# Sixteen-head sparse attention: the even heads' probabilities transposed in squares and by DMA, their product with the values one pair later

## The chip, the cores and the metric

One core of a Trainium2 chip runs the whole program. The metric is device time in microseconds (us) of one execution, the median of three runs. TensorE (PE) does the matrix products, with its weight load shown apart (PEld); VectorE (DVE) and ScalarE (ACT) do everything else that touches elements; GpSimd (POOL) and SyncE (SP) here only start transfers.

## The reference

Two layers and a last norm over x (512 tokens by 2048). Layer 0 is a causal convolution beside a block attention of 8 heads (MoBA). Layer 1 is the sparse attention (DSA) that the change is in:

```python
    q = (cq @ w_qb).reshape(b, t, DSA_HEADS, DSA_HEAD_DIM)
    q_lat = jnp.einsum('bthd,hdc->bthc', q, w_uk)
...
        score = jnp.where(kpos[None, :] <= qpos[:, None], score, -jnp.inf)
        sel = lax.top_k(score, k_top)[1]
...
        p = jax.nn.softmax(s.astype(jnp.float32), axis=-1).astype(kv.dtype)
        return jnp.einsum('bqhk,bqkc->bqhc', p, kv)
...
    o = jnp.einsum('bthc,hcd->bthd', o_lat, w_uv).reshape(b, t, DSA_WIDTH)
    return (o * jax.nn.silu(gate)) @ w_out
```

There are 16 heads of 128, 512 tokens, 128 selected keys for each query. All is in float32.

## The kernel before

Every float32 product is three products of rounded halves (`mm3`, lines 87 to 89): high by low, low by high, high by high. Each operand of one is split by `split` (lines 96 and 97): ACT rounds it to the high part, DVE subtracts for the low part. Weights are loaded by SP in 256 KB pieces and split the same way.

The order of instructions on each engine is fixed at build time. The code gives each piece a due time with `at(t)`, and a planner takes, at each moment of its own simulated clock, the ready instruction with the earliest due time; on the chip each engine then goes through its queue in that order, so an instruction that waits holds up all behind it. Tiles come from pools of a few buffers by tag (`BUFS`): `C` has 8, three of them held by the selection masks, `u` 4, `pt` 7, `A1`, `A2` and `Y` 16 each. The PSUM tags have 2 (`g`), 2 (`s`), 3 (`x`) and 1 (`o`) banks.

The DSA stage goes through 8 pairs of heads, 2 D = 19.8 us of due time each (lines 722 to 769). A pair projects the values v for both heads (24 products 256 wide, two tiles split into four `A2` tiles), then for each head k (6 products 512 wide) and q (12), and calls `attention` (line 223): in four chunks c of 128 queries, scores against 128 (c + 1) keys, the mask and row minimum on DVE (line 238), the exponential with its sum on ACT (line 240), a reciprocal and the normalising multiply on DVE (lines 241, 242), and 10 transposes of 128 by 128 on PE into PSUM (line 249). Three PSUM banks are split into `pt` tiles, and `mm3` takes their product with v (`pso`). The result is multiplied by the head's gate (line 765) and split into `Y` and `A1` tiles, which the last matrix (`w_out2`) reads.

The MoBA stage already has a second way for 7 of its 8 heads, `turned` and `turned_values` (lines 267 to 312): DVE transposes each chunk in 32 by 32 squares into the tile `turn0` (line 286), 16 DMAs of 64 KB started from POOL move the squares to their places in `turn1` (line 290), and one head later `turned_values` splits `turn1` on ACT and DVE and multiplies by v. There is one `turn0` and one `turn1`. The first ACT instruction of that split is made to wait for a named matmul (`behind`).

Of the kernel before, what the change touches and what calls it, by code (L numbers as in the profile page):

```python
# [7 lines left out]
F32R = mybir.dt.float32r  # L8
I32 = mybir.dt.int32
AF = mybir.ActivationFunctionType  # L10
OP = mybir.AluOpType
# [3 lines left out]
P = 128  # L15
# [8 lines left out]
HO = 16  # L24
# [15 lines left out]
def f32(ap):  # L40
    return ap.bitcast(F32)


class Builder:
# [219 lines left out]
            self.mm3(po[:, j * P:], vh, vl, parts[b][0][:, o:o + n], parts[b][1][:, o:o + n], j == 0, j == NT - 1)  # L264
        return po

    def turned(self, q, k, bias, ts):


        nc = self.nc  # L270
        z, y = self.turn
        for c in range(NT):
            w = P * (c + 1)
            self.at(ts(c))
            ps = self.psum("s")
            cs = slice(c * P, (c + 1) * P)
            self.mm3(ps[:, :w], q[0][:, cs], q[1][:, cs], k[0][:, :w], k[1][:, :w], True, True)
            p = self.s("u")
            mn, sm = self.s("col", (P, 1)), self.s("col", (P, 1))
            nc.vector.tensor_tensor_reduce(out=p[:, :w], in0=ps[:, :w], in1=bias(c), scale=1.0, scalar=-OUT,  # L280
                                           op0=OP.add, op1=OP.min, accum_out=mn)
            nc.scalar.activation(p[:, :w], p[:, :w], AF.Exp, bias=mn, scale=-1.0, accum_out=sm)
            nc.vector.reciprocal(sm, sm)
            nc.vector.tensor_scalar(p[:, :w], p[:, :w], sm, None, op0=OP.mult)

            nc.vector.transpose(z[:, :, c, :c + 1, :], p[:, :w].rearrange("p (j b x) -> p b j x", b=4, x=32))  # L286

        for a in range(4):
            for b in range(4):
                nc.gpsimd.dma_start(y[32 * b:32 * (b + 1), a], z[32 * a:32 * (a + 1), b])  # L290
# [171 lines left out]
    def values(self, g, tags=("gg", "xx")):  # L462

        out = []
        for b in range(2):
            t0 = self.t
            ps = [self.psum(tag) for tag in tags[b]]
            for k in range(KC):
                wh, wl = self.weights(self.d["w_v"][g, k], t0 + 1.3 * k)
                self.at(t0 + 1.3 * k)  # L470
                xh, xl = self.xs[k]
                for i in range(2):
                    cs = slice((2 * b + i) * P, (2 * b + i + 1) * P)
                    self.mm3(ps[i], xh[:, cs], xl[:, cs], wh, wl, k == 0, k == KC - 1)
            self.t = t0 + 1.3 * KC
            self.at(self.t)
            for i in range(2):
                j = 2 * b + i
                vh, vl = self.s("G", dt=F32R), self.s("G", dt=F32R)
                self.split(ps[i], vh, vl, self.rcol[:, j:j + 1])  # L480
                out.append((vh, vl))
        return out
# [135 lines left out]
    def odd(self):  # L618
        nc, d = self.nc, self.d
# [4 lines left out]
        ps = self.gemm(d["w_ikw"], self.xs, m=m)  # L624
# [4 lines left out]
        for c in range(NT):  # L629
# [10 lines left out]
                                       op0=OP.mult, op1=OP.mult)  # L640
# [4 lines left out]
        ilh, ihl = self.s("T", dt=F32R), self.s("T", dt=F32R)  # L645
# [4 lines left out]
        h0, zh = self.s("T", dt=F32R), self.s("T", dt=F32R)  # L650
# [5 lines left out]
        gates = []  # L656
# [12 lines left out]
        for i in range(HI // 2):  # L669

            ps = self.gemm(d["w_iq"][i], [(a[:, KTOP:], b[:, KTOP:]) for a, b in cq], n=T - KTOP)
            for e in range(2):
                h = 2 * i + e
# [6 lines left out]
                for c in range(1, NT):  # L680
                    w = P * (c + 1)
# [9 lines left out]
                    else:  # L691
                        nc.vector.scalar_tensor_tensor(sc[c][:, :w], rl[:, :w], iw[:, c, h:h + 1], sc[c][:, :w],
                                                       op0=OP.mult, op1=OP.add)
# [23 lines left out]
        def bias(c):  # L717
            return self.cmask[:, T - P:] if c == 0 else sc[c][:, :P * (c + 1)]

        self.ys = []  # L720
        D = 9.9
        for pair in range(HO // 2):
            t0 = self.t
            wv, wk, wq0, wq1 = [self.weights(d["w_qk"][pair, :, 512 * i:512 * (i + 1)], t0 + (0, 2.6, 3.9, 12.5)[i])
                                for i in range(4)]
            self.at(t0)
            v = []
            for b in range(2):
                ps = self.psum("g")
                for a in range(2):  # L730
                    c = 2 * b + a
                    for k in range(2):
                        cs = slice(c * P, (c + 1) * P)
                        ws = slice(256 * k, 256 * (k + 1))
                        self.mm3(ps[:, 256 * a:256 * (a + 1)], ckv[k][0][:, cs], ckv[k][1][:, cs],
                                 wv[0][:, ws], wv[1][:, ws], k == 0, k == 1)
                vh, vl = self.s("A2", dt=F32R), self.s("A2", dt=F32R)
                self.split(ps, vh, vl)
                v.append((vh, vl))
            for e in range(2):  # L740
                h = 2 * pair + e
                th = t0 + D * e + (0 if e else 2.6)
                parts = []
                for i, (w, xs, o) in enumerate(((wk, ckv, 256 * e), ((wq0, wq1)[e], cq, 0))):
                    self.at(th + 1.3 * i)
                    ps = self.psum("g")
                    for k in range(len(xs)):
                        ws = slice(o + P * k, o + P * (k + 1))
                        self.mm3(ps, w[0][:, ws], w[1][:, ws], xs[k][0], xs[k][1], k == 0, k == len(xs) - 1)
                    zh, zl = self.s("A2", dt=F32R), self.s("A2", dt=F32R)  # L750
                    if i:
                        nc.scalar.activation(zh, ps, AF.Copy, scale=-SCALE)
                        nc.vector.scalar_tensor_tensor(zl, ps, -SCALE, f32(zh), op0=OP.mult, op1=OP.subtract)
                    else:
                        self.split(ps, zh, zl)
                    parts.append((zh, zl))
                k, q = parts

                def vj(j):
                    o = 256 * (j % 2) + P * e  # L760
                    return v[j // 2][0][:, o:o + P], v[j // 2][1][:, o:o + P]

                po = self.attention(q, k, vj, bias, lambda c: th + 6.5 + 1.2 * c, lambda c: th + 12 + 1.2 * c, th + 19, "C")
                y = self.s("tmp")
                nc.vector.tensor_tensor(y, po, gates[h], op=OP.mult)
                yh, yl = self.s("Y", dt=F32R), self.s("A1", dt=F32R)
                self.split(y, yh, yl)
                self.ys.append((yh, yl))
            self.t = t0 + 2 * D

    def final(self):
# [145 lines left out]
```

## Time and profile before

| | us |
|---|---|
| median of three runs | 1522.16 |
| lowest and highest | 1520.82, 1522.37 |
| profiled execution, its own time | 1521.33 |
| its span, first to last instruction | 1519.5 |
| start of the first and of the last gate multiply of the DSA pairs (line 765) | 1186.9, 1344.6 |

The 1.83 us between the span and the profiled time lie outside the instructions. The pairs run from about 1160 us to 1345 us of the span; before them the selection masks are made, and after them comes the product with `w_out2`.

### The profile page before, as it was taken

Reading aid. Unit: us, or ns where it says so; the run is one execution under the profiler, and the core shown is the slowest. Engines: PE = TensorE matmul, PEld = TensorE weight load, DVE = VectorE, ACT = ScalarE, POOL = GpSimd, SP = SyncE. Lnnn points to the kernel's source line nnn. Section 1 sums busy time; section 2 is a strip of 40 time slices with the busy share of each in tenths; the row PEclk is TensorE's granted clock in tenths of the full one; section 3 lists DMA queues with packets and bytes.
Section 4 is the critical chain, followed back from the end, with each engine's and each line's share of the span. In section 5 each row is a group of like instructions: output and inputs, shape, how many; then the busy total and the mean of one; then the engine's idle time right before and its main releaser. Section 6 shows DMA issues by size and latency. Waiting matters only on the chain.

```text
span 1519.5 us, 20122 instructions
## 1 busy us (share of the span) xinstructions
PE 1504.2 (99%) x7137; PEld 1261.3 (83%) x7137; DVE 1018.8 (67%) x1980; ACT 677.5 (45%) x1219; POOL 55.5 (4%) x117
## 2 busy tenths in 40 slices
PE   9999999999999999999999999999999999999996
PEld 7888888888888888888888887788888889888886
DVE  7799999976576645664444445557995898843344
ACT  7533333345374534543333333545324666633341
POOL 0000000002022202220000000000000000000000
PEclk9999999999999999999999999999999999999998
DMA  7233333356234733364444332222232111133333
GB/s 234 89 105 114 102 106 102 104 146 173 93 108 132 204 104 115 113 173 138 146 145 145 125 98 85 95 91 78 90 98 91 55 51 49 56 125 118 126 125 112
DMA packets 97397, 173.22 MB, mean 114 GB/s; under 512 B 12112, under 2 KB 18000, under 8 KB 97296
## 3 DMA queue, kind: packets, MB, share of 16 engines
q1 hardware_dynamic: 93280, 164.45, 34.5%
q0 software_dynamic: 3584, 7.35, 1.7%
q8 instruction: 56, 0.92, 0.2%
q14 instruction: 45, 0.37, 0.1%
q10 hardware_dynamic: 432, 0.14, 0.0%
HBM read 153.93 MB, written 10.49 MB: 108 GB/s over the span
## 4 chain that ended last, share of the span: by engine, by line
PE 97%; DMA 1%; DVE 1%; ACT 0%; issue 0%; SPq 0%; DVEq 0%; ACTq 0%
PE psg L87 28%; PE psg L89 28%; PE psg L88 28%; PE psx L87 1%; PE psx L88 1%; PE psx L89 1%; PE psx L249 1%; PE pss L88 1%; PE pss L89 1%; PE pss L87 1%; PE pso L88 1%; PE pso L89 1%; PE pso L87 1%; DMA wr<-in_w_v 1%; DMA C<-in_w_in 0%; PE psx L686 0%
## 5 line engine op out<-in xcount | busy, mean ns | idle before, releaser
L96 ACT ACTIVATE wh<-wr 128x512 fp32r<-128x512 f32 x508 | 319.4, 629 | 652.2 <-PE psg L89 542.1
L97 DVE TENSOR_TENSOR wl<-wr,wh 128x512 fp32r<-128x512 f32 x508 | 348.5, 687 | 296.3 <-ACT wh L96 295.4
L87 PE MATMUL psg<-A,wh 128*128 128x512 f32 (+1 forms) x1328 | 517.0, 390 | 0.2 <-DVE tmp L782 0.2
L88 PE MATMUL psg<-A,wl 128*128 128x512 f32 x1120 | 436.5, 390 | 0.0
L89 PE MATMUL psg<-A,wh 128*128 128x512 f32 x1120 | 436.4, 390 | 0.0
L87 PEld LDWEIGHTS psg<-A,wh 128*128 128x128 f32 (+1 forms) x1328 | 248.7, 187 | 52.8 <-ACT wh L96 0.6
L88 PEld LDWEIGHTS psg<-A,wl 128*128 128x128 f32 x1120 | 209.6, 187 | 44.8 <-issue 0.4
L89 PEld LDWEIGHTS psg<-A,wh 128*128 128x128 f32 x1120 | 209.6, 187 | 44.4 <-issue 0.4
L415 DVE SCALAR_TENSOR_TENSOR C<-u,cst,C 128x512 f32<-128x512 f32 x240 | 170.0, 745 | 0.2
L89 PE MATMUL psg<-Y,wh 128*128 128x512 f32 x336 | 130.9, 390 | 0.0
L88 PE MATMUL psg<-Y,wl 128*128 128x512 f32 x336 | 130.9, 390 | 0.0
L290 POOL DMA_DIRECT2D turn<-turn x112 | 55.0, 499 | 609.0 <-DVE turn L286 459.4
L88 PEld LDWEIGHTS psg<-Y,wl 128*128 128x128 f32 x336 | 63.0, 188 | 13.0
L89 PEld LDWEIGHTS psg<-Y,wh 128*128 128x128 f32 x336 | 63.1, 188 | 12.8
L87 PE MATMUL psg<-T,wh 128*128 128x512 f32 x160 | 62.6, 391 | 0.0
L88 PE MATMUL psg<-G,wl 128*128 128x512 f32 (+1 forms) x160 | 60.7, 379 | 0.0
L89 PE MATMUL psg<-G,wh 128*128 128x512 f32 (+1 forms) x160 | 60.6, 379 | 0.0
L87 PE MATMUL psg<-Y,wh 128*128 128x512 f32 x128 | 49.8, 389 | 0.0
L240 ACT ACTIVATE C<-C,col 128x128 f32<-128x128 f32 (+1 forms) x64 | 35.8, 560 | 15.6 <-DVE col L238 15.2
L87 PE MATMUL psg<-G,wh 128*128 128x512 f32 (+1 forms) x96 | 36.2, 377 | 0.0
L87 PEld LDWEIGHTS psg<-T,wh 128*128 128x128 f32 x160 | 30.0, 188 | 6.1 <-DVE A L97 0.2
L89 PEld LDWEIGHTS psg<-G,wh 128*128 128x128 f32 x160 | 30.1, 188 | 5.1
(316 smaller groups left out, 2137.0 us busy)
## 6 DMA issues: line engine op xcount, KB each, us to landing
wr<-in_w_in SPq DMA_DIRECT2D x268, 256.0 KB, 3.0
wr<-in_w_out SPq DMA_DIRECT2D x128, 256.0 KB, 2.9
wr<-in_w_v SPq DMA_DIRECT2D x64, 256.0 KB, 2.9
wr<-in_w_qk SPq DMA_DIRECT2D x32, 256.0 KB, 2.4
turn<-turn POOLq DMA_DIRECT2D x112, 64.0 KB, 3.9
Y<-in_xT SPq DMA_DIRECT2D x16, 256.0 KB, 5.1
wr<-in_w_pw SPq DMA_DIRECT2D x16, 256.0 KB, 2.9
tmp<-in_xT SPq DMA_DIRECT2D x16, 256.0 KB, 3.0
```

The source lines that it names most:

```text
L87: i = mm(ps, lh, rl, start=start, stop=False)
L88: mm(ps, ll, rh, start=False, stop=False)
L89: mm(ps, lh, rh, start=False, stop=stop)
L96: i = nc.scalar.activation(th, src, AF.Copy)
L97: nc.vector.tensor_tensor(tl, src, f32(th), op=OP.subtract)
L240: nc.scalar.activation(p[:, :w], p[:, :w], AF.Exp, bias=mn, scale=-1.0, accum_out=sm)
L249: nc.tensor.transpose(px[b][:, o:o + P], p[:, j * P:(j + 1) * P], self.ident)
L290: nc.gpsimd.dma_start(y[32 * b:32 * (b + 1), a], z[32 * a:32 * (a + 1), b])
L415: nc.vector.scalar_tensor_tensor(y, u[:, i:i + T], self.c("w_dw", n * TAPS + i), y, op0=OP.mult, op1=OP.add)
```

## The change

In pairs 0 to 6 the first head of the pair (heads 0, 2, ... 12) takes the `turned` way. Its normalising multiply is done by ACT in place of DVE, then DVE transposes squares into `turn0` and 16 DMAs from POOL move them to `turn1`. Its product with v, the gate and the split of the result come in the next pair, due at t0 + 15 (the split at t0 + 13), behind the k projection of that pair's second head. Pair 7 keeps `attention` for both heads, and also takes the product of head 12.

Since v of a pair is now read in the next pair, v goes in turn to four tiles of tag `T` left from the indexer and to four `u` tiles. The results of the first eight finished heads go to `A1`, of the others to `Y`. The second head's projections now stand ahead of the first head's attention in the program text; the due times of both are as they were.

```diff
-    def turned(self, q, k, bias, ts):
+    def turned(self, q, k, bias, ts, ptag="u", scalar=False):
...
-            nc.vector.tensor_scalar(p[:, :w], p[:, :w], sm, None, op0=OP.mult)
+            if scalar:
+                nc.scalar.activation(p[:, :w], p[:, :w], AF.Copy, scale=sm)
+            else:
+                nc.vector.tensor_scalar(p[:, :w], p[:, :w], sm, None, op0=OP.mult)
...
+        places = [[ilh, ihl, h0, zh], [self.s("u", dt=F32R) for _ in range(4)]]
+        self.ys = [None] * HO
+        left = 2 * HO
...
+            yh, yl = [self.s("A1" if left > HO else "Y", dt=F32R) for _ in range(2)]
...
-                vh, vl = self.s("A2", dt=F32R), self.s("A2", dt=F32R)
+                vh, vl = places[pair % 2][2 * b:2 * b + 2]
...
+                    if not i:
+                        self.mid = ins.ins.name
...
+            values = lambda v, e: lambda j: [x[:, 256 * (j % 2) + P * e:][:, :P] for x in v[j // 2]]
+            if late:
+                po = self.turned_values(values(late, 0), t0 + 15, self.mid)
+                finish(2 * pair - 2, po)
+            late = v if pair < HO // 2 - 1 else None
+            for e in range(2):
+                h = 2 * pair + e
+                th = t0 + D * e + (0 if e else 2.6)
+                k, q = qk[e]
+                if late and e == 0:
+                    self.turned(q, k, bias, lambda c: th + 6.5 + 1.2 * c, "C", True)
+                    continue
+                po = self.attention(q, k, values(v, e), bias, lambda c: th + 6.5 + 1.2 * c,
+                                    lambda c: th + 12 + 1.2 * c, th + 19, "C")
+                finish(h, po)
```

## Rows read from the trace of the kernel before

**Rows 1.** The page: busy time by engine, and the chain that ended last.

```profile
PE 1504.2 (99%) x7137; PEld 1261.3 (83%) x7137; DVE 1018.8 (67%) x1980; ACT 677.5 (45%) x1219; POOL 55.5 (4%) x117
...
PE 97%; DMA 1%; DVE 1%; ACT 0%; issue 0%; SPq 0%; DVEq 0%; ACTq 0%
```

**Rows 2.** Stretch, us, busy of PE, PEld, DVE, ACT, POOL; clock, DMA, GB/s.

```profile
1181.00:1301.00 120.00, 120.00 (x738) 107.62 (x737) 107.04 (x296) 79.15 (x193) 0.00 (x0) 1.00 0.16 52
1281.00:1301.00 20.00, 20.00 (x123) 17.74 (x122) 18.63 (x51) 13.55 (x34) 0.00 (x0) 1.00 0.17 54
```

**Rows 3.** Waits from 1161 to 1345 us: total, times, longest; DVE's eight, and PEld's.

```profile
DVE tmp L765 <- PE pso L89: 10.6, 8, 2.7
...
DVE pt L97 <- ACT pt L96: 0.4, 2, 0.2
...
PEld psg L87 <- DVE A L97: 0.4, 2, 0.2
```

**Rows 4.** PE's timeline (start, us, name, count) around transposes, and without them.

```profile
1249.12 0.95 PE L249 MATMUL psx<-ident,C 128*128 128x128 f32 x7
1249.82 0.31 PE L87 MATMUL pss<-A,A 128*128 128x128 f32 x1
1249.96 0.28 PE L88 MATMUL pss<-A,A 128*128 128x128 f32 x1
...
1269.92 0.22 PE L87 MATMUL pso<-pt,A 128*128 128x128 f32 x1
1269.98 0.27 PE L88 MATMUL pso<-pt,A 128*128 128x128 f32 x1
```

**Rows 5.** PE's timeline: the first k product of pair 1 and of pair 6.

```profile
1177.72 0.39 PE L87 MATMUL psg<-T,wh 128*128 128x512 f32 x1
...
1280.86 0.39 PE L87 MATMUL psg<-T,wh 128*128 128x512 f32 x1
1281.09 0.39 PE L88 MATMUL psg<-T,wl 128*128 128x512 f32 x1
```

**Rows 6.** Groups by line, 1161 to 1345 us: busy us, mean ns, idle before.

```profile
L97 DVE TENSOR_TENSOR pt<-psx,pt 128x512 fp32r<-128x512 f32 (+1 forms) x48 | 27.9, 594 | 0.4 <-ACT pt L96 0.4
...
L242 DVE TENSOR_SCALAR C<-C,col 128x128 f32<-128x128 f32 (+1 forms) x64 | 23.8, 381 | 0.8
L96 ACT ACTIVATE pt<-psx 128x512 fp32r<-128x512 f32 (+1 forms) x48 | 23.6, 523 | 6.1 <-PE psx L249 6.0
```

**Rows 7.** Groups by line in the MoBA stage, 340 to 690 us.

```profile
L286 DVE STREAM_TRANSPOSE turn<-u 128x128 f32<-128x128 f32 (+3 forms) x28 | 14.2, 507 | 0.3
...
L97 DVE TENSOR_TENSOR pt<-turn,pt 128x512 fp32r<-128x512 f32 (+3 forms) x28 | 12.7, 484 | 0.6 <-ACT pt L96 0.5
L96 ACT ACTIVATE pt<-turn 128x512 fp32r<-128x512 f32 (+3 forms) x28 | 11.9, 458 | 3.4 <-PE psg L87 3.4
```

**Rows 8.** POOL's timeline: two batches of 16 moves; then their row of DMA issues.

```profile
469.81 1.47 POOL L290 DMA_DIRECT2D turn<-turn  x3 [28.35 <-DVE turn L286]
471.55 6.36 POOL L290 DMA_DIRECT2D turn<-turn  x13 [0.27 <-issue]
...
621.53 3.92 POOL L290 DMA_DIRECT2D turn<-turn  x8 [26.43 <-issue]
...
628.97 2.45 POOL L290 DMA_DIRECT2D turn<-turn  x5 [0.37 <-issue]
...
turn<-turn POOLq DMA_DIRECT2D x112, 64.0 KB, 3.9
```

**Rows 9.** Timelines of pairs 4 and 5: normalising multiplies, second head's last k group.

```profile
1253.21 0.54 DVE L242 TENSOR_SCALAR C<-C,col 128x128 f32<-128x128 f32 x2
...
1258.39 0.48 DVE L242 TENSOR_SCALAR C<-C,col 128x512 f32<-128x512 f32 x1
...
1268.09 0.48 PE L87 MATMUL psg<-T,wh 128*128 128x512 f32 x1
...
1275.65 0.28 DVE L242 TENSOR_SCALAR C<-C,col 128x128 f32<-128x128 f32 x1
```

More of the change, by code (lines that the diff above doesn't have):

```diff
@@ L277, in turned @@
             self.mm3(ps[:, :w], q[0][:, cs], q[1][:, cs], k[0][:, :w], k[1][:, :w], True, True)
-            p = self.s("u")
+            p = self.s(ptag)
             mn, sm = self.s("col", (P, 1)), self.s("col", (P, 1))
@@ L718, in bias, with finish @@
             return self.cmask[:, T - P:] if c == 0 else sc[c][:, :P * (c + 1)]
-        self.ys = []
+        places = [[ilh, ihl, h0, zh], [self.s("u", dt=F32R) for _ in range(4)]]
+        self.ys = [None] * HO
+        left = 2 * HO
+        def finish(h, po):
+            nonlocal left
+            y = self.s("tmp")
+            nc.vector.tensor_tensor(y, po, gates[h], op=OP.mult)
+            yh, yl = [self.s("A1" if left > HO else "Y", dt=F32R) for _ in range(2)]
+            left -= 2
+            self.split(y, yh, yl)
+            self.ys[h] = (yh, yl)
+        late = None
         D = 9.9
@@ L736, in odd @@
                                  wv[0][:, ws], wv[1][:, ws], k == 0, k == 1)
-                vh, vl = self.s("A2", dt=F32R), self.s("A2", dt=F32R)
+                vh, vl = places[pair % 2][2 * b:2 * b + 2]
                 self.split(ps, vh, vl)
                 v.append((vh, vl))
+            qk = []
             for e in range(2):
@@ L748, in odd @@
                         ws = slice(o + P * k, o + P * (k + 1))
-                        self.mm3(ps, w[0][:, ws], w[1][:, ws], xs[k][0], xs[k][1], k == 0, k == len(xs) - 1)
+                        ins = self.mm3(ps, w[0][:, ws], w[1][:, ws], xs[k][0], xs[k][1], k == 0, k == len(xs) - 1)
+                    if not i:
+                        self.mid = ins.ins.name
                     zh, zl = self.s("A2", dt=F32R), self.s("A2", dt=F32R)
@@ L756, in odd @@
                     parts.append((zh, zl))
[L757 to L768, printed above, removed]
+                qk.append(parts)
+            values = lambda v, e: lambda j: [x[:, 256 * (j % 2) + P * e:][:, :P] for x in v[j // 2]]
[13 more added lines that the diff above has]
+                finish(h, po)
             self.t = t0 + 2 * D
```

## The prediction

> **What bounds the kernel now.** I read the page first: which engine is busy, and who owns the chain that ended last. PE is busy 99% of the span and owns 97% of that chain [rows 1]. An average says nothing of one stage, so next come the stretches of the DSA pairs: from 1181 to 1301 us PE is busy 120.00 of 120.00 us at full granted clock [rows 2]. The waits of the stage say the same from the other side: PE's weight load waited 0.4 us for DVE in 184 us, and everything else in the list is an engine that waits for PE or for its own inputs [rows 3]. So PE's queue sets the time here, and a product taken out of it moves the end by its pitch, as long as nothing else becomes late. The engine to watch is DVE: busy 107.04 of 120 us, 89%, and 93% in the densest 20 us, there too without a PE stall [rows 2]. ACT has 66%, POOL nothing.
>
> A pair takes (1280.86 - 1177.72) / 5 = 20.63 us [rows 5].
>
> **What is removed from PE.** Seven heads lose 10 transposes each. A record's length (0.27 us) overlaps its neighbours, so I take start to start: seven transposes move the next product by 1249.82 - 1249.12 = 0.70 us, and the narrow product behind them keeps the one after it waiting 0.14 us where it takes 0.06 us without transposes ahead [rows 4]. That is 0.78 us for seven, 0.11 us each, 1.1 us a head and **7.7 us** for seven heads. The products with v and the scores keep their shapes, they only change places: head 0's values leave pair 0, head 12's enter pair 7. Nothing is added to PE.
>
> **What is added to DVE and ACT**, for each turned head. Out of DVE go four normalising multiplies, 4 x 0.381 = 1.52 us, and three splits from PSUM, 3 x 0.594 = 1.78 us [rows 6]. Into it come four square transposes, 4 x 0.507 = 2.03 us, and four splits of the moved squares, 4 x 0.484 = 1.94 us [rows 7], priced on the same shapes in the MoBA stage. Net +0.67 us. A pair has 0.892 x 20.63 = 18.4 us of DVE now, 19.1 us after, in 20.63 - 1.1 = 19.5 us: 98%. These busy times count the tail of each instruction, which the next one overlaps, so the true fill is lower; still it is the least cover in this change. ACT loses 3 x 0.523 = 1.57 us [rows 6] and gains four splits, 4 x 0.458 = 1.83 us [rows 7], and four multiplies that the trace doesn't show; bounded by 0 and by the 0.523 us of a PSUM split, I take 0.458 us, the nearest in shape, 1.83 us. Net +2.1 us a pair on 0.66 x 20.63 = 13.6 us: 80% full, not a bound by itself.
>
> **The moves.** One head's 16 moves are issued in 477.91 - 469.81 = 8.1 us at best and 631.42 - 621.53 = 9.9 us at worst of these two batches, and the last lands a median 3.9 us later [rows 8]: 12 to 14 us. Nothing else is in POOL's queue in the pairs [rows 2], so no issue is moved past another there; SP's queue keeps its weight loads. The added traffic is 1 MB a pair beside 52 GB/s [rows 2], another 1 MB / 19.5 us = 54 GB/s; I cost it at nothing, since loads are due 8 us ahead. If that cover were gone, a weight split would be late, and PE with it.
>
> What waits on the moves is the tight place. In pair 4 the first head's last normalising multiply ends at 1258.87 us [rows 9]. After the change an ACT multiply and a transpose stand there, about 1.3 us more, so POOL starts near 1260.7 and the squares are landed at 1273 to 1275. Two instructions of pair 5 need that. The split on ACT may start once the k group at 1268.09 us has run [rows 9], 1.1 us earlier with the shorter pair, so 1267: the guard by itself lets it go 6 to 8 us too soon. Only the planner's own idea of a landing, and the due time t0 + 13 behind more urgent work, keep it back. And the first transpose of pair 5 overwrites the tile that the moves read; its place is that of the multiply at 1275.65 us [rows 9], about 1274.8 after: just as the moves end, with -0.2 to 1.8 us to spare. Behind a DVE instruction that waits there stand the weight splits that PE needs next.
>
> The buffers: v now lives in tiles that no one else uses in the pairs, and `Y` slots come free with the gates, two for each head finished. I cost these at nothing; the work that would be late if I am wrong is the split of v, which PE needs last in the pair.
>
> **The sum.** PE -7.7 us. For new stalls I take 0 to 0.2 us for each of six pairs as the likeliest, +0.7 us: the densest stretch ran at 93% of DVE without one [rows 2]. The profiled 1521.33 us (its span 1519.5 us and 1.83 us around it) becomes 1514.3 us, and the median, 0.83 us above it, 1515.1 us. This case's own range: 1514.0 (no stall, and transposes in small groups cost a little more than 0.11 us) to 1518.
>
> **Rival 1: DVE becomes the bound.** DVE now waits 28.9 us in 184 us (eight rows [rows 3], the greatest 10.6 us for the product with v), 3.2 us in each pair. With 19.1 us of work in 19.5 us these waits must almost vanish. Most do by themselves, since an engine that lags finds its inputs ready. If 1 us a pair stays, the pair takes 20.1 us, and of 1.1 us saved 0.5 us is left: 7 x 0.5 = 3.5 us, 1518.7 us. If 1.5 us stays nothing is left, 1522 us. The Trainium skill speaks for this rival: VectorE: DVE Perf Modes, section Rules for kernel authors, advises TensorE for a 128 by 128 transpose if PSUM will do as its destination. The pitch here bears out that TensorE's way is the cheaper one for each block; the rule leaves out that PE is the scarce engine.
>
> **Rival 2: the split is queued too early; slower.** If the planner puts ACT's split right behind the guard at 1267 us, ACT stands until 1273 to 1275, 7 us in the middle. Behind it are the evictions of the second head's k and q and the weight splits. PE can go on with what is already split, the second head's q (12 products, 1281.09 - 1280.86 = 0.23 us each [rows 5], 2.8 us) and the rest of a product with v or of the scores, by estimate 4 to 5 us in all; then it stands 2 to 3 us in each of 7 pairs, +14 to +21 us against -7.7 us: 1528 to 1535 us, 1530 in the middle. It decides from about 4.5 us of ACT wait; under 5.5 us or so the pair still breaks even. For it: the rows above. Against it: the due time puts the split at 13 of a pair's 19.8 us, behind the scores and exponentials that are due from 9.1 us on, and in the MoBA stage the same split idled 3.4 us for PE and for no move [rows 7], though with more time between the heads than a pair gives.
>
> A slower issue would feed the same rival. The trace has 6.36 us for 13 issues, 0.49 us each, in a stage where such multiplies run on DVE too [rows 8]. The Trainium skill (SBUF — State Buffer, section SBUF: two separate sides) says that VectorE's two-port instructions lock GpSimd out while it writes descriptors. By that rule the second head's four multiplies a pair could stretch a batch by up to their 1.5 us; the sum above holds without it, since the 9.9 us batch already lies inside the bounds.
>
> **Rival 3: the change does what it says, but PE waits where it worked.** Stalls of 0.7 to 1.5 us a pair from a mixture of the tight transposes and DVE's queue take back nearly all: 1519.2 to 1525 us.
>
> **How the numbers follow.** The likeliest: 0.50. Rival 1 with something left: 0.15. Rival 3, or rival 1 with nothing left: 0.15. Rival 2: 0.20. A measurement of this kernel can tell 0.2%, 3.0 us, from no change. Faster by more than that: the likeliest case, and most of rival 1's remainder, 0.63. Within it: the rest of rival 1 and most of rival 3, 0.17. Slower: rival 2, 0.20. The range goes from 1513.5 us (7.7 us, a larger pitch, and the 0.8 us by which runs differ) up to 1528 us, the lower end of rival 2, which leaves out about 0.15 above and under 0.05 below.
>
> **What would show it.** Right: the transposes of line 249 in the pairs fall from 160 to 90, the pair's period to 19.5 us, PE stays at 20.00 of 20 us, and the waits of PE in the stage remain under 1.5 us. DVE above 95% with PE waits for `wl` or `A` is rival 1. ACT `pt` waits for `turn`, or a DVE transpose that waits for a DMA, with PE idle a few us behind the k group, is rival 2. The prediction is wrong if PE's idle time in the stage exceeds 3 us, or if the 70 transposes return less than 1 us a head although PE is full.

## The result, and the profile after

The changed kernel is slower: **1539.79 us** median of four runs (1536.45 to 1540.76), where the kernel before, measured again beside it, has 1521.49 us (1520.24 to 1522.37). The ratio is 1.0119, with an interval of 1.0106 to 1.0131. The forecast was 1515.1 us, faster, with a range up to 1528 us: wrong in sign, and outside its range.

The profiled execution took 1540.49 us, its span 1538.7 us: 19.2 us more than the span before. On the page of the changed kernel, busy time by engine and the chain that ended last (before: [rows 1]):

```profile
PE 1509.8 (98%) x7067; PEld 1257.1 (82%) x7067; DVE 1020.5 (66%) x1987; ACT 691.8 (45%) x1254; POOL 111.8 (7%) x229
...
PE 95%; DVE 3%; DMA 1%; issue 1%; ACT 0%; DVEq 0%; SPq 0%; ACTq 0%
```

PE has its 70 transposes less (7137 to 7067) and is busy longer all the same, 1509.8 against 1504.2 us. Outside its busy time it stands 1538.7 - 1509.8 = 28.9 us, before 1519.5 - 1504.2 = 15.3 us. So the 19.2 us are 13.6 us of idling and 5.6 us of longer work. The stretches of the pairs, in the columns of [rows 2], show where:

```profile
1181.00:1301.00 120.00, 109.41 (x595) 91.42 (x594) 96.66 (x273) 81.20 (x197) 44.78 (x90) 0.96 0.34 94
...
1201.00:1221.00 20.00, 19.44 (x102) 17.39 (x103) 15.31 (x40) 12.18 (x27) 8.07 (x16) 0.88 0.32 86
1221.00:1241.00 20.00, 18.12 (x98) 15.22 (x97) 16.16 (x48) 14.17 (x37) 8.21 (x16) 1.00 0.37 100
...
1281.00:1301.00 20.00, 17.54 (x102) 14.69 (x101) 17.82 (x52) 14.40 (x37) 4.98 (x11) 1.00 0.29 84
```

PE was full before and has 109.41 of 120 us now, and in some stretches less than the full granted clock (0.96 in the mean, 0.88 in one). DVE did not fill up: 96.66 of 120 us, 81%, less than before. Every engine has slack, so what is late is an order or a buffer, not an engine. The pair's period says the same by another way. The first k product of pair 1 and of pair 6, as in [rows 5]:

```profile
1177.68 0.39 PE L87 MATMUL psg<-T,wh 128*128 128x512 f32 x1
...
1298.31 0.47 PE L87 MATMUL psg<-T,wh 128*128 128x512 f32 x1 [1.00 <-DVE T L97]
```

(1298.31 - 1177.68) / 5 = 24.1 us a pair instead of 20.63, and the second line names a releaser that PE did not have before: `T` written by line 97 is v in its new place. The waits from 1161 to 1370 us (total, times, longest; [rows 3] has PE's 0.4 us of before):

```profile
PEld pso L87 <- DVE pt L97: 6.0, 10, 1.2
PE pso L87 <- DVE pt L97: 5.4, 6, 2.9
...
PEld pss L87 <- DVE col L238: 4.4, 5, 1.4
...
PEld psg L87 <- issue: 3.7, 3, 1.2
...
ACT T L96 <- PE pso L89: 1.9, 2, 1.3
```

PE waits for `pt`, the split of the moved squares, in front of the late product (`pso`); for the mask and row minimum of the other head (`col`, line 238), which hold a bank that its scores need; and at the start of the next pair (`psg`). The last line is v's split, which waits for the late product to release the place that it is to be written to.

**The late split and the late transposes.** POOL's batch that starts at 1249 us, and the first instructions behind it, from the timelines of POOL, ACT and DVE:

```profile
1249.07 0.50 POOL L293 DMA_DIRECT2D turn<-turn  x1 [14.34 <-DVE col L241]
1249.94 7.62 POOL L293 DMA_DIRECT2D turn<-turn  x15 [0.37 <-issue]
...
1266.80 0.62 ACT L96 ACTIVATE pt<-turn 128x512 fp32r<-128x512 f32 x1
...
1267.30 1.10 DVE L289 STREAM_TRANSPOSE turn<-C 128x128 f32<-128x128 f32 x3 [0.21 <-issue]
```

The row of DMA issues from 1181 to 1301 us (count, size, median us from issue to landing):

```profile
turn<-turn POOLq DMA_DIRECT2D x90, 64.0 KB, 2.0
```

The last move is issued by 1249.94 + 7.62 = 1257.6 us and lands some 2.0 us later: the squares are there by about 1260 us, and by 1261.8 us even with the longest landing in the pairs, 4.2 us. The second head's k products, one of which guards the split, had run too; this is the last of them:

```profile
1258.18 0.39 PE L89 MATMUL psg<-T,wh 128*128 128x512 f32 x1
```

Yet ACT's split starts at 1266.80 us, 17.7 us behind the first move (16.2 to 18.6 us over the seven batches). Neither ACT nor DVE waits for a landing anywhere in the list of waits; only POOL does, once, for 0.5 us. So the order of the queues has put the split there, behind the next head's softmax. The next head's square transposes stand in the same place, since with one `turn0` they may not come before the moves either: three in one record at 1267.30 us, though the first two of ACT's multiplies (line 285) had ended at 1263.9 us. Softmax, transposes and two splits come in one bunch per pair, the batch of moves follows, and the next bunch waits behind it in the order. POOL's batches start at 1180.75 and, six pairs on, at 1319.73 us, 23.2 us apart.

**The clock.** Three stretches had the granted clock at half, which is the 1.2 of the levels 1.2 and 2.4 GHz:

```profile
1199.00:1205.80 6.80, 4.24 (x16) 3.94 (x17) 5.98 (x18) 3.49 (x9) 2.42 (x5) 0.50 0.09 19
1250.20:1253.60 3.40, 3.40 (x10) 2.35 (x10) 2.95 (x7) 1.22 (x5) 3.40 (x7) 0.50 0.51 121
1321.80:1325.30 3.50, 3.43 (x10) 2.78 (x11) 1.90 (x5) 0.73 (x2) 3.50 (x8) 0.51 0.60 131
```

PE worked 4.24 + 3.40 + 3.43 = 11.07 us in them. The pitch of a product is 0.43 us there and 0.23 us at the full level (last section), so by estimate 11.07 x (1 - 0.23 / 0.43) = 5.1 us are lost. The first stretch begins 0.4 us into PE's longest wait (from 1201.56 - 2.92 = 1198.64 us); the other two stand behind several short waits, of which these are the last:

```profile
1201.56 0.76 PE L87 MATMUL pso<-pt,T 128*128 128x512 f32 x1 [2.92 <-DVE pt L97]
...
1248.83 0.39 PE L87 MATMUL pso<-pt,T 128*128 128x256 f32 x1 [0.89 <-DVE pt L97]
...
1321.87 0.76 PE L87 MATMUL psg<-T,wh 128*128 128x512 f32 x1 [1.00 <-DVE u L97]
```

Before the change no stretch of the pairs was below 1.00.

### The profile page after: what moved, and what is told of

It reads as the page before. It is cut to its first block, busy times and chain, and to the rows that moved or that the text cites. A ratio compares the mean times of both kernels' runs of the same rounds, so it can differ in the third digit from the quotient of the medians.

```text
span 1538.7 us, 20215 instructions
## 1 busy us (share of the span) xinstructions
PE 1509.8 (98%) x7067; PEld 1257.1 (82%) x7067; DVE 1020.5 (66%) x1987; ACT 691.8 (45%) x1254; POOL 111.8 (7%) x229
## 4 chain that ended last, share of the span: by engine, by line
PE 95%; DVE 3%; DMA 1%; issue 1%; ACT 0%; DVEq 0%; SPq 0%; ACTq 0%
PE psg L87 28%; PE psg L88 27%; PE psg L89 27%; PE psx L87 2%; PE psx L88 2%; PE psx L89 2%; PE pss L88 1%; PE pss L89 1%; PE pss L87 1%; PE pso L89 1%; PE pso L88 1%; PE pso L87 1%; PE psx L249 1%; DVE pt L97 1%; DVE turn L289 1%
## 5 line engine op out<-in xcount | busy, mean ns | idle before, releaser
L88 PE MATMUL psg<-A,wl 128*128 128x512 f32 (+1 forms) x1224 | 477.2, 390 | 0.0
L89 PE MATMUL psg<-A,wh 128*128 128x512 f32 (+1 forms) x1224 | 476.9, 390 | 0.0
L87 PE MATMUL psg<-A,wh 128*128 128x512 f32 (+1 forms) x1224 | 476.4, 390 | 0.2 <-DVE tmp L807 0.2
L87 PEld LDWEIGHTS psg<-A,wh 128*128 128x128 f32 (+1 forms) x1224 | 229.1, 187 | 49.1 <-ACT wh L96 0.6
L88 PEld LDWEIGHTS psg<-A,wl 128*128 128x128 f32 (+1 forms) x1224 | 229.1, 187 | 48.5 <-issue 0.4
L89 PEld LDWEIGHTS psg<-A,wh 128*128 128x128 f32 (+1 forms) x1224 | 229.1, 187 | 48.4 <-issue 0.4
L293 POOL DMA_DIRECT2D turn<-turn x224 | 111.3, 504 | 1215.3 <-DVE col L241 590.3
L88 PE MATMUL psg<-Y,wl 128*128 128x512 f32 x232 | 90.3, 389 | 0.0
L87 PEld LDWEIGHTS psg<-Y,wh 128*128 128x128 f32 x232 | 43.6, 188 | 9.0
L89 PEld LDWEIGHTS psg<-Y,wh 128*128 128x128 f32 x232 | 43.6, 188 | 9.0
L88 PEld LDWEIGHTS psg<-Y,wl 128*128 128x128 f32 x232 | 43.5, 188 | 8.9
L87 PEld LDWEIGHTS psg<-T,wh 128*128 128x128 f32 x160 | 30.5, 191 | 10.5 <-issue 3.7
```

Source lines behind the costliest of these rows:

```text
L87: i = mm(ps, lh, rl, start=start, stop=False)
L88: mm(ps, ll, rh, start=False, stop=False)
L89: mm(ps, lh, rh, start=False, stop=stop)
```

## Experiments

Two causes were open after the traces. **L**: the split and the next transposes come too late in the order. **V**: v of a pair goes to the place that the late product of the pair in progress still reads (two places, three pairs alive), so PE can't run ahead into the next pair. Rivals were DVE as the bound (**D**), and the new places and text order by themselves. The kernels are made from the changed one; the times of the kernel before beside them were 1521.1 to 1521.6 us.

**No head turned.** The new places, tags and order of the text stay, the turning goes.

```diff
-            late = v if pair < HO // 2 - 1 else None
+            late = None
```

> No head of the sparse attention is turned, none comes late; what stays of the change is the places of v, the tags of the results and the order of the program text. All theories that put the cost on the turning (L, D) expect the time of the kernel before, 1520 to 1523 us. If the new places or the new order cost something by themselves it is above 1525 us.

1520.56 us (1519.90 to 1523.24), ratio 0.9997 (0.9987 to 1.0006); PE is full:

```profile
1181.00:1301.00 120.00, 120.00 (x739) 107.84 (x738) 105.74 (x294) 78.88 (x191) 0.00 (x0) 1.00 0.15 51
```

Nothing of the rearrangement costs anything until a head is turned.

**A quarter of the moves.** Of the 16 moves only the 4 on the diagonal are made in DSA; the other 12 are left out, and the product takes what lies there.

```diff
-            for b in range(4):
+            for b in ((a,) if scalar else range(4)):
```

> The changed kernel, but each turned head of the sparse attention starts 4 of its 16 moves; the other 12 are left out, so three quarters of the transposed probabilities are old data. All VectorE, ScalarE and TensorE instructions stay. Theory L (loop): with one turn0 and one turn1 the queue order lets neither the next head's square transposes nor the previous head's split begin before the moves are due to be landed, some 17 us after POOL starts them; everything then comes in one bunch per pair and the pair takes 23 us where TensorE needs 19.6. With a quarter of the moves the bunch can spread, the pair falls to 19.6 to 20.5 us and the time to 1514 to 1522 us. Theory D (VectorE's added 0.67 us a head, 98% fill) and theory V (two places for v) change nothing here: 1536 to 1541 us.

1519.87 us (1518.82 to 1522.60), ratio 0.9992 (0.9983 to 1.0002): 19.9 us faster than the changed kernel and no faster than before. The split now starts 11.0 us behind the first move, and the moves of the next pair come 20.6 us later:

```profile
1217.22 1.96 POOL L293 DMA_DIRECT2D turn<-turn  x4 [18.67 <-DVE turn L289]
1237.79 1.96 POOL L293 DMA_DIRECT2D turn<-turn  x4 [18.61 <-DVE col L241]
...
1228.25 0.62 ACT L96 ACTIVATE pt<-turn 128x512 fp32r<-128x512 f32 x1
```

Most of PE's waits that are left come at the first k product, for v in its two kinds of place:

```profile
PE psg L87 <- DVE T L97: 2.7, 3, 0.9
PEld psg L87 <- DVE u L97: 2.0, 3, 0.7
```

**A third place for v.** Four more `A2` tiles, all 16 moves.

```diff
-        places = [[ilh, ihl, h0, zh], [self.s("u", dt=F32R) for _ in range(4)]]
+        places = [[ilh, ihl, h0, zh], [self.s("u", dt=F32R) for _ in range(4)],
+                  [self.s("A2", dt=F32R) for _ in range(4)]]
...
-                vh, vl = places[pair % 2][2 * b:2 * b + 2]
+                vh, vl = places[pair % 3][2 * b:2 * b + 2]
```

> The changed kernel with a third set of four tiles for v (from tag A2), so that v of the next pair never waits for the late product of the last one. Theory V: TensorE's waits behind the split of v (about 1.2 us before the k products of six pairs, 7 us) go, 1531 to 1534 us or better. Theory L and theory D: the bunch is as late as before, 1536 to 1541 us.

1523.60 us (1522.50 to 1525.02), ratio 1.0015 (1.0005 to 1.0024): 16.2 us faster than the changed kernel, more than twice the 7 us of waits that I had put on v's places, and still not faster than before.

```profile
1221.00:1241.00 20.00, 20.00 (x117) 17.64 (x116) 18.43 (x51) 15.65 (x38) 7.82 (x16) 1.00 0.42 119
1241.00:1261.00 20.00, 18.15 (x107) 15.62 (x106) 16.43 (x49) 14.21 (x35) 7.93 (x16) 1.00 0.34 93
```

PE runs ahead for a while and is full up to 1241 us; from then on the late bunches reach it, in waits of at most 1.2 us, and the clock stays at 1.00. The order is still the late one: first move at 1226.77 us, split at 1243.59, 16.8 us behind it (14.5 to 18.8 us over the batches).

**Every other pair turned.** Pairs 0, 2, 4 and 6 alone, so no turned head follows another.

```diff
-            late = v if pair < HO // 2 - 1 else None
+            late = v if pair % 2 == 0 else None
```

> Only pairs 0, 2, 4 and 6 turn their first head; pairs 1, 3, 5 and 7 transpose on TensorE. The loop of moves has two pairs' time. Theory L: no bunching, the 40 transposes taken away return 4 x 1.1 us less small stalls, 1517 to 1522 us. Theory D: the stall belongs to each turned head, so four of seven keep it: of +18 us some 10 remain, 1529 to 1533 us. Theory V (the v of the next pair but one is written where the late product still reads): with a late product only in pairs 1, 3, 5 and 7 the waits halve, 1528 to 1533 us.

1534.40 us (1532.47 to 1535.39), ratio 1.0082 (1.0065 to 1.0099). The number that L alone gave is missed: with four heads in place of seven the loss is 12.8 us of 18.3. D and V, whose ranges ended at 1533 us, come nearer and are missed by 1.4 us; this time alone does not tell the two apart. A batch starts at 1225.66 us and its split, with nothing turned in between, at 1243.79, 18.1 us behind it. Then PE stands for it, here and twice more:

```profile
1245.35 0.77 PE L87 MATMUL pso<-pt,T 128*128 128x512 f32 x1 [3.22 <-DVE pt L97]
```

```profile
1244.70:1251.50 6.80, 6.15 (x23) 5.69 (x24) 5.70 (x12) 4.39 (x10) 0.00 (x0) 0.50 0.00 0
```

So the lateness is not only that of a loop from one turned head to the next; the place of the split in the order is late by itself, and with v's place taken PE has nothing to do meanwhile. The clock falls to half inside this wait, which began at 1245.35 - 3.22 = 1242.13 us, and stays there for 6.8 us.

**Both at once.** The next two kernels take away L and V together: once with a quarter of the moves (12 of 16 left out), once with all 16 and a complete computation, the moves issued by SyncE instead of GpSimd. Both have the third place.

```diff
-                nc.gpsimd.dma_start(y[32 * b:32 * (b + 1), a], z[32 * a:32 * (a + 1), b])
+                (nc.sync if scalar else nc.gpsimd).dma_start(y[32 * b:32 * (b + 1), a], z[32 * a:32 * (a + 1), b])
```

> A quarter of the moves (12 of 16 left out, as before) and a third place for v, together. Theory L+V (the late landing in the queue order, and the v of the pair after that may not be written until the late product has read its place, so that TensorE's queue has nothing to run ahead with): each alone left 10 to 14 us of stalls, both together leave under 3 us, and the 7.7 us of the transposes come out: 1513 to 1516 us. Theory D (VectorE too full): with all its instructions still there TensorE goes on waiting for VectorE, 1518 us or more.

> All 16 moves, started by SyncE in place of GpSimd, and a third place for v. The reference is computed whole. Theory L: if the queue order counts a landing from SyncE earlier than one from GpSimd, the loop falls under the 19.6 us of a pair and the time comes to 1513 to 1518 us; if the order counts it no earlier, 1522 to 1525 us as with the third place alone. Against it: the moves stand in the queue of the weight loads, and a load that waits behind them would show as ScalarE waiting for wr. Theory D: 1518 us or more in any case.

1514.07 us (1513.64 to 1514.71) and 1514.06 us (1513.77 to 1514.65), both with a ratio of 0.9952 (0.9937 to 0.9967). **The second one beats both kernels.** The stretch of the pairs with a quarter of the moves, the same with SyncE, and the page of the SyncE kernel:

```profile
1181.00:1301.00 120.00, 120.00 (x713) 107.02 (x712) 110.98 (x317) 94.87 (x236) 10.41 (x21) 1.00 0.22 66
```

```profile
1181.00:1301.00 120.00, 119.97 (x711) 106.82 (x710) 110.16 (x316) 94.78 (x236) 0.00 (x0) 1.00 0.39 106
```

```profile
PE 1496.6 (99%) x7067; PEld 1254.0 (83%) x7067; DVE 1018.7 (67%) x1987; ACT 690.6 (46%) x1254; POOL 55.4 (4%) x117
```

PE is busy 1496.6 us of a span of 1512.2: 7.6 us less than before, and it stands 15.6 us where it stood 15.3. That is what the 70 transposes were priced at. The added traffic is no cause of the loss either: this kernel moves more in the stretch than the changed one, 106 against 94 GB/s, with PE full. SyncE is the slower issuer, 11.3 us for this batch; but the split comes 13.05 us behind the first move instead of 17.7 (12.4 to 14.4 us over the seven batches, against 16.2 to 18.6):

```profile
1199.11 11.29 SPq L293 DMA_DIRECT2D turn<-turn  x16
...
1212.16 0.64 ACT L96 ACTIVATE pt<-turn 128x512 fp32r<-128x512 f32 x1 [0.48 <-DMA turn<-turn]
1212.23 0.64 DVE L289 STREAM_TRANSPOSE turn<-C 128x128 f32<-128x128 f32 x2
```

Here the split does wait for the landing, 0.48 us, which costs PE nothing. With data that lands later and a split that comes earlier, the lateness in the changed kernel was the order's, not the transfer's. Why the order is so is argued, not shown: the planner's own clock seems to count a batch from GpSimd as landed much later than the chip lands it.

**SyncE with two places.** The same moves, v's places as in the change: the late order off, V on.

> All sixteen moves of the seven even heads are issued by SyncE instead of GpSimd; v keeps its two places, as in the changed kernel. The computation is complete. Theory LV (two causes that multiply: the bunched order behind GpSimd's moves, and v written where the late product still reads): only the first is taken away, so this should stand near the kernel with a quarter of the moves, 1518 to 1522 us, with stalls of about 1 us before the next pair's first k product in several pairs, none of 3 us, and no stretch of half clock. Rival S (who issues the moves is all that matters, and the third place did nothing in the kernel that had both): 1514 us, with TensorE 120.0 of 120 us busy in 1181 to 1301. Rival V (the places for v are the whole loss): 1533 us or more, with stalls of about 3 us and half clock.

1527.14 us (1525.95 to 1528.18), ratio 1.0037 (1.0024 to 1.0051). None of the three expectations: the third place is worth 13.1 us with SyncE, so S is out; it is 6 us under V's number, so V is not the whole; and 1518 to 1522 us with no stretch of half clock, which I gave for what V leaves, is 5 us too low, and the clock was at half in two stretches, the one shown below and another from 1288.70 us. The trace has what I had left out:

```profile
PEld psx L249 <- DVE C L242: 6.8, 5, 2.0
PEld psg L87 <- issue: 4.8, 5, 2.2
...
DVE turn L289 <- DMA turn<-turn: 3.9, 2, 2.3
```

```profile
1200.00:1203.20 3.20, 3.20 (x9) 2.54 (x8) 2.27 (x6) 1.19 (x3) 0.00 (x0) 0.50 0.44 103
```

DVE waits up to 2.3 us for the slower batch, and PE's longest row is the transposes of the other head, which wait for DVE's multiplies. The chain that ended last ties the two together (start, us, what):

```profile
1251.24 3.30 DMA turn<-turn
1254.96 0.64 DVE turn L289 x2
...
1273.58 3.78 DMA turn<-turn
1277.44 0.64 DVE turn L289 x2
...
1287.80 0.47 PE psg L87
```

From SyncE's moves at 1241.97 us to PE's first k product at 1287.80 us this chain holds moves, landings and the work of DVE and ACT, and no product. With one `turn0` the next transposes may not come before the last moves have landed, so here the loop of moves is closed by the transfer itself and not by the order. In the kernel with three places the same batches cost PE nothing; I take it that PE has the lead there to cover them.

**Half the moves from each queue,** eight from GpSimd and eight from SyncE, with the third place.

```diff
+                (nc.sync if scalar and b % 2 else nc.gpsimd).dma_start(y[32 * b:32 * (b + 1), a], z[32 * a:32 * (a + 1), b])
```

> Eight moves from GpSimd, eight from SyncE, and a third place for v; computed whole. Theory L: the batch is issued in half the time (8.2 to 4.1 us on GpSimd), the loop shortens by at least 4 us from 22.9 to under 19.6 us: 1513 to 1518 us. Theory D: 1518 us or more.

1516.15 us (1515.41 to 1517.59), ratio 0.9966 (0.9953 to 0.9979). PE is busy 120.00 of 120 us in the pairs. In the profiled execution, the slowest of the five with 1517.59 us, one wait at their end, with half clock behind it from 1343.0 to 1346.2 us, goes with the rest:

```profile
1342.85 0.74 PE L87 MATMUL psg<-Y,wh 128*128 128x512 f32 x1 [1.89 <-DVE Y L97]
```

That is the split of a finished head in front of `w_out2`. Issuing faster gains nothing once PE is full.

**DVE loaded again.** A quarter of the moves (12 of 16 left out), three places, and the normalising multiply back on DVE.

```diff
-                    self.turned(q, k, bias, lambda c: th + 6.5 + 1.2 * c, "C", True)
+                    self.turned(q, k, bias, lambda c: th + 6.5 + 1.2 * c, "C", False, True)
```

(The last argument selects the quarter of the moves.)

> As with a quarter of the moves and the third place, and the normalising multiply of the turned heads back on VectorE: 4 x 0.381 = 1.52 us more of VectorE in each turned pair, 1.8 us less of ScalarE. It measures how much room VectorE has. Theory D: VectorE's work comes to about the 19.6 us of the pair and TensorE waits for it, 4 to 10 us more than without. Theory L+V: VectorE's back-to-back work is 2.5 us under the pair before and has room for it, within 2 us of the run without.

1516.79 us (1514.30 to 1517.09), ratio 0.9964 (0.9950 to 0.9978).

```profile
1181.00:1301.00 120.00, 120.00 (x710) 106.94 (x709) 114.89 (x334) 83.46 (x209) 11.21 (x23) 1.00 0.23 70
```

That is 2.7 us more than without, between the two expectations (within 2 us, or 4 to 10 us more). DVE is at 114.89 of 120 us, 96%, and PE has no gap in the pairs, so D is out as the bound there. What is lost in the profiled execution is again one wait of 2.17 us for `Y` in front of `w_out2`, at 1341.86 us, and half clock behind it from 1343.2 to 1346.4 us.

The runs that vary moves and places, in us:

| moves of a head | two places for v | three places | the third is worth |
|---|---|---|---|
| 16 from GpSimd | 1539.79 | 1523.60 | 16.2 |
| 16 from SyncE | 1527.14 | 1514.06 | 13.1 |
| 4 from GpSimd | 1519.87 | 1514.07 | 5.8 |

Neither cause explains the loss alone: with two places a late bunch hits PE at once, with three it must first eat up PE's lead. Not tried: a second pair of `turn` tiles, which would let the transposes run ahead of the moves and the split.

## Why the prediction was wrong, step by step

**The bound: right.** PE's queue set the time, and where nothing is late its 70 transposes are worth 7.6 us, by the page of the SyncE kernel, for the 7.7 us of the sum. [rows 4] priced them well, start to start.

**DVE and ACT: small errors, with no effect.** The groups of the changed kernel from 1161 to 1345 us that answer [rows 7], and ACT's multiply, which [rows 6, 7] had to bound:

```profile
L285 ACT ACTIVATE C<-C,col 128x128 f32<-128x128 f32 (+3 forms) x28 | 15.0, 555 | 2.5 <-DVE col L283 2.3
L97 DVE TENSOR_TENSOR pt<-turn,pt 128x512 fp32r<-128x512 f32 (+3 forms) x28 | 12.7, 478 | 0.0
L289 DVE STREAM_TRANSPOSE turn<-C 128x128 f32<-128x128 f32 (+3 forms) x28 | 12.5, 487 | 0.7 <-issue 0.4
L96 ACT ACTIVATE pt<-turn 128x512 fp32r<-128x512 f32 (+3 forms) x28 | 11.7, 455 | 0.0
```

Transposes and splits are within 5% of their prices; the multiply takes 0.555 us, above the upper bound of 0.523. The sum said 98% for DVE; where PE is full it is 92% (110.98 and 110.16 of 120 us), and a load of 96% was still no bound. So rival 1 fell. The rule of the Trainium skill that it leaned on (VectorE: DVE Perf Modes, section Rules for kernel authors: TensorE for a 128 by 128 transpose, if PSUM will do) would have kept the slower kernel here: in the SyncE kernel DVE's way wins 0.48%, with PE the scarce engine.

**The moves: somewhat quicker than said.** A batch took 8.0 to 8.5 us of POOL, the lower end of [rows 8], and landed 2.0 us later, not 3.9: some 10.5 us in place of 12 to 14. The stretching by DVE that the Trainium skill describes (SBUF — State Buffer, section SBUF: two separate sides) did not appear: the batch that starts at 1273.18 us has all four multiplies of the second head beside it and takes 7.97 us, the least of the seven. The issues beside the pairs' DVE work, min/median/max in ns:

```profile
L293 POOL DMA_DIRECT2D turn<-turn x112: 496/498/733, 1180.7 to 1327.2; - x112
```

**The tight place: the first step that failed, right in its place and wrong in its sign.** The prediction compared a guard at 1267 us with a landing at 1273 to 1275 and asked who would wait for the DMA. In the changed kernel neither ACT nor DVE did. Rival 2 let the planner queue the split 7 us too early; it queued it about 7 us too late (1260 against 1266.80 us). "Only the planner's own idea of a landing [...] keep it back" named the unknown, but only one of its sides was priced. The transposes were given "-0.2 to 1.8 us to spare" by their old places; in the new order they moved together with the split, 18.2 us behind the first move. By the columns of the table the late order costs 12.7 us (against SyncE) to 19.9 us (against 4 moves) with two places for v, and 9.5 us with three.

**The buffers: the second step that failed.** "v now lives in tiles that no one else uses in the pairs" is true, and does not make it free: the other user is v itself, two pairs on. A late product in pair p reads the place that pair p + 1's v is written to, and those projections come soon behind it in PE's queue. "I cost these at nothing; the work that would be late if I am wrong is the split of v" names the wait that the trace then showed. But PE did not need it "last in the pair": v's two products fill both `g` banks of PSUM, and the first k product right behind them waits for one of these to be split (`psg`, the 1.00 us waits shown above). The price of having two places and not three is the last column of the table: 5.8 to 16.2 us.

**New stalls: the term that was mis-sized.** The sum took 0 to 0.2 us a pair, 0.7 us in all. Against the SyncE kernel the changed one has 28.9 - 15.6 = 13.3 us more idling and 1509.8 - 1496.6 = 13.2 us more busy time; by the estimate above 5.1 us of the latter is half clock, and the other 8.1 us, perhaps products that lengthen where they come one by one behind waits, I can't assign to rows. The prediction had no term for the clock at all, although it counted stalls of 0.7 to 3 us in its rivals, and waits of 0.89 to 2.92 us went with half clock here.

**The case and the range.** The nearest case was rival 3 (PE waits where it worked) by mechanism and rival 2 by time. Rival 3's 0.7 to 1.5 us a pair was read from a mixture of small delays; the idling alone came to 13.3 / 7 = 1.9 us a pair, the clock and the stretched products to as much again. The range ended at 1528 us, rival 2's lower end, and left out its whole middle; 1539.79 us lies above even rival 2's upper end, 1535 us.

## What to carry to other kernels

When a product is put off by one round, count the places of every operand that it still reads, against the rounds alive at once: with one place too few the next round's producer waits for the late consumer, and the engine that was full loses its lead. When an order is planned ahead, price a DMA that the planner thinks too slow as well as one that it thinks too fast; on the trace the former is work that starts long after its data landed, with no wait for a DMA anywhere. A saving of PE time must be counted with the clock that its new gaps cost.

## What the runs showed of the hardware

- The granted clock went to half for 6.8 us around a wait of PE of 2.92 us in the changed kernel and one of 3.22 us in the run with every other pair. It also did so for 3.4 and 3.5 us behind waits of 0.89 and 1.00 us, and with SyncE and two places for 3.2 and 3.3 us behind waits of 1.79 and 1.57 us. In the kernel with three places and GpSimd, whose waits in the pairs were 1.2 us at most, it was 1.00 throughout. So the length of one wait does not tell whether the clock will fall. At half clock the same product has a pitch of 1252.07 - 1251.64 = 0.43 us, where [rows 5] has 0.23:

```profile
1251.64 0.63 PE L89 MATMUL psg<-T,wh 128*128 128x512 f32 x1
1252.07 0.63 PE L87 MATMUL psg<-T,wh 128*128 128x512 f32 x1
```

- SyncE issues these moves more slowly than GpSimd: 588 ns in the median and 10.0 to 11.3 us for 16, against 498 ns and 8.0 to 8.5 us; landing took a median of 2.0 us from either.
- With eight moves from each of the two queues, the batch at 1239 us took 5.19 us on SyncE and 4.04 us on GpSimd, side by side: about half a full batch of each. Landing took a median of 3.0 and 2.7 us there.
